# Output and down projections in five column pieces of 410 and 408 instead of four of 512

## The chip, the core and the metric

The kernel runs on one core of a Trainium2 chip. The metric is the device time of one execution in microseconds (us), as the median of several runs. Next to it stands one profiled execution, from which all the rows below come. The engines are called PE (TensorE, the matrix multiplier), ACT (ScalarE), DVE (VectorE), POOL (GpSimd) and SP (SyncE, which issues the transfers of the weights); PEld is the part of TensorE that loads the stationary operand.

## The reference

Two layers of an encoder work on x, 256 rows of 2048 columns in float32. Cut to what matters here, one layer is

```python
h = rms_norm(x, attn_norm[l])
proj = jnp.einsum('bsd,de->bse', h, w_in[l])        # 2048 -> 4672 columns
...                                                 # three mixers a, b, c of 4, 6 and 6 heads of 128
y = jnp.concatenate([rms_norm(ya, g_a), rms_norm(yb, g_b), rms_norm(yc, g_c)], axis=-1)
x = x + jnp.einsum('bse,ed->bsd', y, w_out[l])      # 2048 -> 2048
h = rms_norm(x, ffn_norm[l])
ff = jax.nn.silu(h @ w_gate[l]) * (h @ w_up[l])     # 2048 -> 5632, twice
x = x + ff @ w_down[l]                              # 5632 -> 2048
```

After the second layer a last rms_norm with the gain final_norm gives the output.

## The kernel before

**Units.** Every projection is cut into units (line 350). A unit is one weight matrix, a range of contraction tiles of 128 rows (`k0`, `nk`) and a range of output columns (`c0`, `n`, at most 512). `run_units` (line 353) works through all units of both layers in one list. It cuts a unit into granules of two contraction tiles, and a granule into twelve matmuls: each float32 weight is split into a high part `wh` and a low part `wl`, each activation likewise (`xh`, `xl` or `ah`, `al`), and of the four products three are kept, for two contraction tiles and two halves `t` of the 256 rows (lines 424 to 431). The stationary operand of a matmul is a 128x128 tile of activations, the moving operand a weight tile of `n` columns, and the result goes to `acc`, of which there are two sets. A new stationary tile is loaded for every matmul.

**Weights.** One load brings up to four contraction tiles of a unit (`load`, line 365) into one of three `raw` buffers, by SP's queue. `convert` (line 380) makes `wh` by a cast on ACT and `wl` by a subtraction on DVE, two granules ahead of the matmuls, into three buffers; the next load is issued when the last granule of a `raw` buffer is converted.

**Ends of units.** When a unit's last matmul has been issued, its evacuation waits for the next granule's conversion to be issued (`pend`, lines 411 to 413) and then runs: for the output projection (`ev_out`, line 878) and the down projection (`ev_down`, line 945) DVE adds `acc` to the columns of x, once for each `t`.

**The rest of the work** (attention, norms, transposes) is made of tasks. `pump` (line 215) puts them between the granules, by a planner's own costs and due times (`Pace`, line 37); what is ordered there at build time is the order on the engines. A norm of x is taken in four chunks of 512 columns (`norm_chunk`, line 328): each is transposed on PE, scaled and split on ACT and DVE, and squared on ACT. The norm before the gate and up projections starts from `ev_out` of mixer b (`m == 1`, the last of the three), the norm before the second layer from `ev_down` of the last group; the final norm instead takes each piece as it comes (`final_part`, line 332): squares on ACT, then a multiplication by the gain on DVE.

**Sizes of what the change touches.** The output projection has 4, 6 and 6 contraction tiles for the three mixers, in the order a, c, b (line 888), each with four column pieces. The down projection has 44 contraction tiles in six groups, five of 8 and one of 4, each with four column pieces. In the second layer the last group has five, since its last 512 columns are cut in two (lines 968 and 969).

Of the kernel before, what the change touches and what calls it, by code (L numbers as in the profile page):

```python
# [13 lines left out]
ALU = mybir.AluOpType  # L14
# [6 lines left out]
D = 2048  # L21
DEPTH = 2
# [8 lines left out]
MAX_HEADS = 5  # L31
PE_SLACK = -800
READY_AHEAD = 250
QUEUE_AHEAD = 3000


# [80 lines left out]
def hybrid_encoder(tc, pools, a, out):  # L117
    pace = Pace()
    nc = Core(tc.nc, pace)
# [5 lines left out]
    gf = [None, None]  # L125
# [6 lines left out]
    x = const.tile([P, T, D], F32, name="x")  # L132
# [23 lines left out]
    def drop(name, i):  # L156
        slots[name].append((pace.mark, i))
# [17 lines left out]
    def temp(name, shape, dtype=F32):  # L175
        i = yield from take(name)
        return i, sp.tile(shape, dtype, name=f"{name}{i}", tag=f"{name}{i}", bufs=1)
# [10 lines left out]
    def finish(key):  # L188
        done[key] = pace.mark + Pace.HOP
# [15 lines left out]
    def due(task):  # L205
        now = pace.at["pe"]
        if task.engine == "pe":
            return task.ready <= now + PE_SLACK
        return task.ready <= now + READY_AHEAD and pace.at.get(task.engine, 0.0) <= now + QUEUE_AHEAD

# [35 lines left out]
    def start(gen, engine="pe", ready=None):  # L246
        prep.append(Task(gen, engine, max(pace.at["act"], pace.at["dve"]) + Pace.HOP if ready is None else ready))
# [11 lines left out]
    def inv_rms(dst, ss, width, n):  # L259
        ms = tiny.tile([P, 16], F32, name="ms", tag="ms", bufs=2)  # L260
        nc.vector.tensor_scalar(ms[:, :n], ss, 1.0 / width, EPS, ALU.mult, ALU.add)
        nc.gpsimd.tensor_tensor(dst, ms[:, :n], half[:, :n], ALU.pow)

    def small(name, n, bufs=2):
        return tiny.tile([P, n], F32, name=name, tag=name, bufs=bufs)
# [15 lines left out]
    def new_norm(gbase, key):  # L281
        n = Norm()
        n.gbase, n.key = gbase, key
        n.hi = [None] * 8
        n.lo = [None] * 8
        n.ss = tiny.tile([P, 10 if key == "final" else 8], F32, name=f"ss_{key}")
        n.parts = 0
        n.r = tiny.tile([P, 2], F32, name=f"r_{key}")
        n.left = 8
        return n  # L290
# [6 lines left out]
    def norm_end(n):  # L297
        tot = small("tot", 2)
        nc.vector.tensor_reduce(tot, n.ss.rearrange("p (t c) -> p t c", t=T), AX.X, ALU.add)
        inv_rms(n.r, tot, D, 2)  # L300
        finish((n.key, "r"))

    def norm_pair(n, kp):
        n.hi[kp] = sp.tile([P, 2, S], F32R, name=f"xh{kp}", tag=f"xh{kp}", bufs=1)
        n.lo[kp] = sp.tile([P, 2, S], F32R, name=f"xl{kp}", tag=f"xl{kp}", bufs=1)
        bank = yield from grab()
        for j in range(2):
            kt = 2 * kp + j
            for t in range(T):
                o = j * S + t * P  # L310
                nc.tensor.transpose(bank[1][:, o : o + P], x[:, t, kt * P : (kt + 1) * P], ident)
        yield "act"
        g = gT[:, n.gbase + 2 * kp : n.gbase + 2 * kp + 2]
        split_scaled(
            [(n.hi[kp][:, j], n.lo[kp][:, j], bank[1][:, j * S : (j + 1) * S], g[:, j : j + 1]) for j in range(2)]
        )
        give(bank)
        finish((n.key, kp))
        cur[0].ready += 2000
        yield "act"  # L320
        i, junk = yield from temp("pr", [P, T, S])
        square(n, kp // 2, kp % 2, junk.rearrange("p t s -> p (t s)"))
        drop("pr", i)
        if n.left == 0:
            yield "dve"
            norm_end(n)

    def norm_chunk(n, c, ready=None):
        for b in range(2):
            start(norm_pair(n, 2 * c + b), "pe", ready)  # L330

    def final_part(n, c0, w):
        i, junk = yield from temp("pr", [P, T, S])
        for t in range(T):
            nc.scalar.activation(
                junk.rearrange("p t s -> p (t s)")[:, :w], x[:, t, c0 : c0 + w], AF.Square,
                accum_out=n.ss[:, 5 * t + n.parts : 5 * t + n.parts + 1],
            )
        drop("pr", i)
        n.parts += 1  # L340
        if n.parts == 5:
            norm_end(n)
        for t in range(T):
            xs = x[:, t, c0 : c0 + w]
            nc.vector.tensor_mul(xs, xs, gf[c0 // 1024][:, c0 % 1024 // 512, c0 % 512 : c0 % 512 + w])


    units = []
# [1 line left out]
    def unit(w, k0, nk, c0, n, act, evac, need=None, evac_need=()):  # L350
        units.append((w, k0, nk, c0, n, act, evac, need, evac_need))
# [120 lines left out]
    def layer(l, nrm, next_norm):  # L472
        L = Norm()
# [5 lines left out]
        nh = (A_H, B_H, C_H)  # L479
        y_base = (0, A_H, A_H + B_H)  # L480
# [7 lines left out]
        def y_tiles(kt):  # L488
            i = kt // 8
            if L.y[i] is None:  # L490
                L.y[i] = tuple(
                    sp.tile([P, 8, S], F32R, name=f"a{s}{i}", tag=f"a{s}{i}", bufs=1) for s in "hl"
                )
            return L.y[i][0][:, kt % 8], L.y[i][1][:, kt % 8]
# [380 lines left out]

        fn = new_norm(G_FFN + 16 * l, f"ffn{l}")

        def ev_out(m, c):
            def f(acc):
                for t in range(T):  # L880
                    xs = x[:, t, c * 512 : (c + 1) * 512]
                    nc.vector.scalar_tensor_tensor(xs, acc[t], L.rm[m][:, t : t + 1], xs, ALU.mult, ALU.add)
                if m == 1:
                    norm_chunk(fn, c)

            return f

        for m in (0, 2, 1):
            for c in range(4):
                unit(  # L890
                    a["w_out"][l], y_base[m], nh[m], c * 512, 512,
                    lambda k, b=y_base[m]: y_tiles(b + k), ev_out(m, c),
                    lambda k, b=y_base[m]: ("y", l, b + k), (("rm", l, m),),
                )

# [7 lines left out]
        groups = [(0, 1), (2, 3), (4, 5), (6, 7), (8, 9), (10,)]  # L903
        F = Norm()
# [37 lines left out]

            return f

        def ev_down(g, c, c0, n):
            def f(acc):
                for t in range(T):
                    xs = x[:, t, c0 : c0 + n]
                    nc.vector.tensor_add(xs, acc[t][:, :n], xs)
                if g == len(groups) - 1:  # L950
                    if l + 1 < DEPTH:
                        norm_chunk(next_norm, c)
                    else:
                        start(final_part(next_norm, c0, n), "act")
                elif l + 1 == DEPTH and g == 0 and c == 0:
                    final_gain()

            return f
# [5 lines left out]

        def down(g):
            k0 = 4 * groups[g][0]
            cuts = [0, 512, 1024, 1536, 2048]
            if l + 1 == DEPTH and g == len(groups) - 1:
                cuts.insert(4, 1792)
            for c0, c1 in zip(cuts, cuts[1:]):  # L970
                unit(
                    a["w_down"][l], k0, 4 * len(groups[g]), c0, c1 - c0,
                    lambda k: (F.t[g][0][:, k], F.t[g][1][:, k]), ev_down(g, c0 // 512, c0, c1 - c0),
                    lambda k: ("ff", l, groups[g][0] + k // 4),
                )

        gu(0)
        for g in range(1, len(groups)):
            gu(g)
            down(g - 1)  # L980
        down(len(groups) - 1)


    norms = [new_norm(G_ATTN + 16 * l, f"attn{l}") for l in range(DEPTH)] + [new_norm(0, "final")]
    for l in range(DEPTH):
        layer(l, norms[l], norms[l + 1])
# [17 lines left out]
    def final_gain():  # L1004
        gf[:] = [nat(tag, 512) for tag in ("n2", "n3")]
        for i, g in enumerate(gf):
            src = a["final_norm"].unsqueeze(0)[:, i * 1024 : (i + 1) * 1024].to_broadcast([P, 1024])
            nc.sync.dma_start(g, src.rearrange("p (t n) -> p t n", t=T))
# [16 lines left out]
    for c in range(4):  # L1025
        xs = x[:, :, c * 512 : (c + 1) * 512]
# [72 lines left out]
```

## Time and profile before

| | |
|---|---|
| median of 3 runs | 2220.07 us (2219.35 to 2221.93) |
| the profiled execution's own time | 2221.58 us |
| its span, first to last instruction | 2219.8 us |
| instructions | 26883 |
| PE, DVE, ACT, POOL busy | 99%, 56%, 47%, 9% of the span |
| weights and other data read from memory | 399.50 MB |

A busy share of PE says only that some matmul was in flight, since matmuls overlap: what a matmul costs is read from the distance between the starts of two that follow each other. In a line of the timeline the first column is the start of the first instruction of a run of equal ones, the second the time from there to the end of the last, and "x4" their count; what stands in brackets is how long the engine was idle before, and what ended that.

### The profile page before, as it was taken

What the parts mean: (1) busy time and instruction counts of PE and PEld (TensorE: products, weight loads), DVE (VectorE), ACT (ScalarE), POOL (GpSimd) and SP (SyncE); (2) the same over time, 40 slices, a digit from 0 to 9 for tenths busy, and PEclk for the clock granted to TensorE, in tenths of its full rate; (3) what the DMA queues carried; (4) which work ended last, traced back from release to release, by engine and by line L of the source; (5) the groups of instructions that cost most, each with busy time, mean ns of one, the idle gap of its engine ahead of it and who ended that gap; (6) DMA issues with size and microseconds to landing.
All of it is one profiled execution on the core that took longest, in us unless ns stands there. A gap on an engine that the chain in (4) does not pass through costs nothing.

```text
span 2219.8 us, 26883 instructions
## 1 busy us (share of the span) xinstructions
PE 2192.1 (99%) x10486; PEld 1842.1 (83%) x10486; DVE 1244.8 (56%) x1468; ACT 1045.0 (47%) x1473; POOL 210.3 (9%) x323
## 2 busy tenths in 40 slices
PE   8999999999999999999999999999999999999997
PEld 7887988888888888888888889888888888888886
DVE  5556676444545455455655567664455455554555
ACT  6556545444344443444455555454444434444444
POOL 0425400000000000000004453000000000000000
PEclk9999999999999999999999999999999999999999
DMA  7544466565655555555555535565656556555553
GB/s 263 169 125 146 128 198 194 186 193 189 191 190 189 190 190 190 190 190 190 190 191 166 158 100 166 171 193 191 190 192 208 191 190 190 190 190 190 190 190 133
DMA packets 213295, 403.34 MB, mean 182 GB/s; under 512 B 6848, under 2 KB 28848, under 8 KB 213168
## 3 DMA queue, kind: packets, MB, share of 16 engines
q1 hardware_dynamic: 210416, 399.55, 56.3%
q10 hardware_dynamic: 2752, 2.07, 0.3%
q8 instruction: 82, 1.34, 0.2%
q14 instruction: 45, 0.37, 0.0%
HBM read 399.50 MB, written 2.10 MB: 181 GB/s over the span
## 4 chain that ended last, share of the span: by engine, by line
PE 64%; issue 33%; POOL 1%; DVE 1%; DMA 0%; ACT 0%; ACTq 0%; POOLq 0%; SPq 0%; DVEq 0%
PE acc L95 59%; PE side L95 5%; POOL trig_c L95 0%; DMA gc<-in_c_q_norm_dram 0%; POOL tb L95 0%; POOL ta L95 0%; POOL n L95 0%; DMA gains<-in_attn_norm_dram 0%; DVE wl L95 0%; ACT wh L95 0%; ACT pr L95 0%; DVE pr L95 0%; DVE qkl L95 0%; DVE nm L95 0%; ACT x L95 0%
## 5 line engine op out<-in xcount | busy, mean ns | idle before, releaser
L95 DVE TENSOR_TENSOR wl<-raw,wh 128x1024 fp32r<-128x1024 f32 (+3 forms) x786 | 938.4, 1194 | 822.8 <-ACT wh L95 787.9
L95 ACT CAST wh<-raw 128x1024 fp32r<-128x1024 f32 (+3 forms) x786 | 800.1, 1018 | 957.0 <-PE acc L95 941.3
L95 PE MATMUL acc<-wh,xl 128*128 128x512 f32 (+2 forms) x2112 | 545.3, 380 | 0.0
L95 PE MATMUL acc<-wl,xh 128*128 128x512 f32 (+2 forms) x2112 | 544.7, 380 | 0.0
L95 PE MATMUL acc<-wh,xh 128*128 128x512 f32 (+2 forms) x2112 | 543.5, 379 | 1.1 <-ACT wh L95 1.1
L95 PEld LDWEIGHTS acc<-wh,xh 128*128 128x128 f32 x2112 | 384.4, 189 | 73.6 <-ACT wh L95 1.5
L95 PEld LDWEIGHTS acc<-wh,xl 128*128 128x128 f32 x2112 | 385.6, 189 | 72.1
L95 PEld LDWEIGHTS acc<-wl,xh 128*128 128x128 f32 x2112 | 382.9, 189 | 70.6
L95 PE MATMUL acc<-wl,ah 128*128 128x512 f32 (+2 forms) x1032 | 276.2, 389 | 0.0
L95 PE MATMUL acc<-wh,ah 128*128 128x512 f32 (+2 forms) x1032 | 273.3, 387 | 0.0
L95 PE MATMUL acc<-wh,al 128*128 128x512 f32 (+2 forms) x1032 | 272.8, 386 | 0.0
L95 PEld LDWEIGHTS acc<-wh,al 128*128 128x128 f32 x1032 | 192.6, 188 | 38.7
L95 PEld LDWEIGHTS acc<-wh,ah 128*128 128x128 f32 x1032 | 192.2, 188 | 38.5
L95 PEld LDWEIGHTS acc<-wl,ah 128*128 128x128 f32 x1032 | 189.8, 188 | 35.9
L95 POOL TENSOR_TENSOR r_attn<-ms,half 128x2 f32<-128x2 f32 x2 | 1.4, 700 | 763.2 <-DVE ms L95 763.2
L95 POOL TENSOR_TENSOR r_final<-ms,half 128x2 f32<-128x2 f32 x1 | 0.8, 802 | 720.2 <-DVE ms L95 720.2
L95 ACT CAST ah<-side 128x512 fp32r<-128x512 f32 x44 | 25.8, 587 | 83.1 <-PE side L95 83.1
L95 DVE TENSOR_TENSOR x<-acc,x 128x512 f32<-128x512 f32 (+1 forms) x98 | 61.8, 672 | 1.2 <-PE acc L95 1.2
L95 DVE TENSOR_TENSOR al<-side,ah 128x512 fp32r<-128x512 f32 x44 | 30.4, 692 | 55.0 <-ACT ah L95 55.0
L95 PE MATMUL side<-ident,n 128*128 128x128 f32 x336 | 50.4, 274 | 6.6 <-POOL n L95 6.3
L95 PEld LDWEIGHTS side<-ident,n 128*128 128x128 f32 x336 | 40.4, 139 | 16.1 <-POOL n L95 8.0
L95 POOL TENSOR_TENSOR n<-ta,tb 128x256 f32<-128x256 f32 (+1 forms) x48 | 39.4, 821 | 3.8
(112 smaller groups left out, 958.0 us busy)
## 6 DMA issues: line engine op xcount, KB each, us to landing
raw<-in_w_gate_dram SPq DMA_DIRECT2D x88, 1024.0 KB, 5.1
raw<-in_w_up_dram SPq DMA_DIRECT2D x88, 1024.0 KB, 5.1
raw<-in_w_down_dram SPq DMA_DIRECT2D x87, 1024.0 KB, 5.0
raw<-in_w_in_dram SPq DMA_DIRECT2D x55, 1024.0 KB, 5.0
raw<-in_w_out_dram SPq DMA_DIRECT2D x24, 1024.0 KB, 5.2
raw<-in_w_in_dram SPq DMA_DIRECT2D x26, 512.0 KB, 3.7
raw<-in_w_out_dram SPq DMA_DIRECT2D x16, 512.0 KB, 3.6
raw<-in_w_in_dram SPq DMA_DIRECT2D x8, 640.0 KB, 4.1
```

What stands on the lines that cost most here:

```text
L95: f(*args, **kw)
```

## The change

The output projection and the down projection take their 2048 columns in the pieces 0 to 410, 410 to 820, 820 to 1230, 1230 to 1640 and 1640 to 2048, in every group of both layers. Since the norms still go by chunks of 512 columns, a chunk is started by the piece that completes it (`whole`): the pieces 2, 3, 4 and 5 complete the chunks 1, 2, 3 and 4, and piece 1 completes none. In the final norm, the multiplication by the gain is cut where a piece crosses a multiple of 512.

```diff
+CUTS = (0, 410, 820, 1230, 1640, 2048)
...
+        edges = [c0] + [e for e in range(512, D, 512) if c0 < e < c0 + w] + [c0 + w]
         for t in range(T):
-            xs = x[:, t, c0 : c0 + w]
-            nc.vector.tensor_mul(xs, xs, gf[c0 // 1024][:, c0 % 1024 // 512, c0 % 512 : c0 % 512 + w])
+            for e0, e1 in zip(edges, edges[1:]):
+                xs = x[:, t, e0:e1]
+                nc.vector.tensor_mul(xs, xs, gf[e0 // 1024][:, e0 % 1024 // 512, e0 % 512 : e0 % 512 + e1 - e0])
...
+        def whole(c1, c0):
+            return [c for c in range(4) if c0 < (c + 1) * 512 <= c1]
+
-        def ev_out(m, c):
+        def ev_out(m, c0, n):
             def f(acc):
                 for t in range(T):
-                    xs = x[:, t, c * 512 : (c + 1) * 512]
-                    nc.vector.scalar_tensor_tensor(xs, acc[t], L.rm[m][:, t : t + 1], xs, ALU.mult, ALU.add)
+                    xs = x[:, t, c0 : c0 + n]
+                    nc.vector.scalar_tensor_tensor(xs, acc[t][:, :n], L.rm[m][:, t : t + 1], xs, ALU.mult, ALU.add)
                 if m == 1:
-                    norm_chunk(fn, c)
+                    for c in whole(c0 + n, c0):
+                        norm_chunk(fn, c)
...
         for m in (0, 2, 1):
-            for c in range(4):
+            for c0, c1 in zip(CUTS, CUTS[1:]):
                 unit(
-                    a["w_out"][l], y_base[m], nh[m], c * 512, 512,
-                    lambda k, b=y_base[m]: y_tiles(b + k), ev_out(m, c),
+                    a["w_out"][l], y_base[m], nh[m], c0, c1 - c0,
+                    lambda k, b=y_base[m]: y_tiles(b + k), ev_out(m, c0, c1 - c0),
...
-        def ev_down(g, c, c0, n):
+        def ev_down(g, c0, n):
...
-                        norm_chunk(next_norm, c)
+                        for c in whole(c0 + n, c0):
+                            norm_chunk(next_norm, c)
...
-                elif l + 1 == DEPTH and g == 0 and c == 0:
+                elif l + 1 == DEPTH and g == 0 and c0 == 0:
...
-            cuts = [0, 512, 1024, 1536, 2048]
-            if l + 1 == DEPTH and g == len(groups) - 1:
-                cuts.insert(4, 1792)
-            for c0, c1 in zip(cuts, cuts[1:]):
+            for c0, c1 in zip(CUTS, CUTS[1:]):
                 unit(
                     a["w_down"][l], k0, 4 * len(groups[g]), c0, c1 - c0,
-                    lambda k: (F.t[g][0][:, k], F.t[g][1][:, k]), ev_down(g, c0 // 512, c0, c1 - c0),
+                    lambda k: (F.t[g][0][:, k], F.t[g][1][:, k]), ev_down(g, c0, c1 - c0),
```

## Rows read from the trace of the kernel before

**Rows 1.** The timeline of PE inside a down projection of the first layer.

```profile
597.02 1.07 PE L95 MATMUL acc<-wh,al 128*128 128x512 f32 x4
...
600.64 1.07 PE L95 MATMUL acc<-wl,ah 128*128 128x512 f32 x4
```

**Rows 2.** The timeline of PE: 384-column, 320-column and 256-column pieces.

```profile
85.94 0.85 PE L95 MATMUL acc<-wh,al 128*128 128x384 f32 x4
...
88.71 0.85 PE L95 MATMUL acc<-wl,ah 128*128 128x384 f32 x4
...
251.20 0.75 PE L95 MATMUL acc<-wl,xh 128*128 128x320 f32 x4
251.79 0.75 PE L95 MATMUL acc<-wh,xh 128*128 128x320 f32 x4
...
2203.25 0.64 PE L95 MATMUL acc<-wh,al 128*128 128x256 f32 x4
...
2208.05 0.64 PE L95 MATMUL acc<-wl,ah 128*128 128x256 f32 x4
```

**Rows 3.** The page's costliest groups: matmuls of the projections after the first.

```profile
L95 PE MATMUL acc<-wh,ah 128*128 128x512 f32 (+2 forms) x1032 | 273.3, 387 | 0.0
```

**Rows 4.** Stretches: busy time (instructions) of PE, PEld, DVE, ACT, POOL; PEclk, DMA share, GB/s.

```profile
250.00:280.00 30.00, 30.00 (x247) 29.99 (x246) 23.99 (x48) 19.17 (x44) 17.05 (x23) 1.00 0.50 142
600.00:690.00 90.00, 90.00 (x402) 74.52 (x401) 43.62 (x40) 38.15 (x39) 0.00 (x0) 1.00 0.59 187
```

**Rows 5.** Groups by form: conversions and adds of different widths.

```profile
L95 DVE TENSOR_TENSOR wl<-raw,wh 128x1024 fp32r<-128x1024 f32 x710 | 874.8, 1232 | 776.5 <-ACT wh L95 770.6 <-PE acc L95 4.6
...
L95 ACT ACTIVATE pr<-x 128x512 f32<-128x512 f32 x38 | 24.0, 639 | 0.1
...
L95 DVE TENSOR_TENSOR wl<-raw,wh 128x768 fp32r<-128x768 f32 x8 | 7.7, 962 | 12.3 <-PE acc L95 9.8 <-ACT wh L95 2.5
...
L95 ACT CAST wh<-raw 128x768 fp32r<-128x768 f32 x8 | 6.7, 840 | 10.9 <-PE acc L95 10.8
...
L95 ACT ACTIVATE pr<-x 128x256 f32<-128x256 f32 x4 | 1.7, 418 | 2.1 <-DVE x L95 2.1
```

**Rows 6.** The timeline of ACT in the first layer's output projection (one of an even pattern).

```profile
321.34 1.06 ACT L95 CAST wh<-raw 128x1024 fp32r<-128x1024 f32 x1 [1.66 <-PE acc L95]
```

**Rows 7.** The timeline at the first layer's end, where the next norm's chunks come in.

```profile
1104.26 1.04 PE L95 MATMUL side<-ident,x 128*128 128x128 f32 x8
...
1104.89 1.57 ACT L95 ACTIVATE xh<-side,gT 128x256 fp32r<-128x256 f32 x4 [0.30 <-PE side L95]
...
1105.77 1.28 DVE L95 TENSOR_TENSOR x<-acc,x 128x512 f32<-128x512 f32 x2
...
1106.97 1.65 DVE L95 SCALAR_TENSOR_TENSOR xl<-side,gT,xh 128x256 fp32r<-128x256 f32 x4
```

**Rows 8.** The DMA issues, with KB of one and the median us to landing.

```profile
raw<-in_w_down_dram SPq DMA_DIRECT2D x87, 1024.0 KB, 5.0
...
raw<-in_a_w_uq_dram SPq DMA_DIRECT2D x4, 768.0 KB, 4.4
```

**Rows 9.** The timeline of the end, all engines.

```profile
2208.61 0.76 DVE L95 TENSOR_TENSOR x<-acc,x 128x256 f32<-128x256 f32 x2 [1.21 <-PE acc L95]
2209.07 0.42 ACT L95 ACTIVATE pr<-x 128x256 f32<-128x256 f32 x1 [0.92 <-DVE x L95]
2209.28 0.75 DVE L95 TENSOR_TENSOR x<-x,n 128x256 f32<-128x256 f32 x2
...
2210.15 0.16 DVE L95 TENSOR_REDUCE tot<-ss_final 128x2 f32<-128x10 f32 x1
...
2210.42 0.76 DVE L95 TENSOR_TENSOR x<-x,n 128x256 f32<-128x256 f32 x2
2210.59 0.80 POOL L95 TENSOR_TENSOR r_final<-ms,half 128x2 f32<-128x2 f32 x1 [720.24 <-DVE ms L95]
```

**Rows 10.** A stretch of the second layer's attention, columns as in the stretches above.

```profile
1255.00:1300.00 45.00, 39.70 (x239) 34.95 (x237) 25.61 (x48) 26.65 (x74) 26.92 (x48) 0.92 0.51 167
```

## The prediction, made before the changed kernel ran

> **What bounds the kernel now.** I began with the busy shares of the page: PE is busy nearly all of the span, every other engine about half of it or less. That alone proves little, since overlapping matmuls keep PE "busy" even where it starts them late. So the second view is the timeline of PE, and in it the distance between starts. In a down projection with pieces of 512 columns, 16 matmuls lie between the two starts shown: 3.62 us, 226 ns each to the rounding of the rows [rows 1]. The other widths in this kernel give 2.77 us for 16 at 384 columns (173 ns), 0.59 us for 4 at 320 (147 to 148 ns) and 4.80 us for 40 at 256 (120.0 ns) [rows 2]. These four lie on one line: from 256 to 512 columns the step grows by 106.7 ns, which is 0.4167 ns a column, one column per cycle at 2.4 GHz; what is left at zero columns is 120.0 - 106.7 = 13.3 ns. The line gives 226.7, 173.3, 146.7 and 120.0. So **each matmul costs its columns and 13.3 ns more, whatever its width**. In the 90 us window the granted clock is 1.00 and PE is busy all through [rows 4]; ACT's conversions of weights stand idle before each start until a matmul frees their buffer, 1.66 us out of each 2.72 us [rows 6]. The supply waits for PE, not PE for the supply. In the stretches that the change touches, time is therefore the number of matmuls times their step.
>
> **The matmuls, removed and added.** One form of the three products counts 1032 matmuls outside the w_in, gate and up projections [rows 3]. By the code that is 2 layers x 2 halves x (16 tiles x 4 pieces of w_out + 44 x 4 of w_down + 16 of the low-rank projections) = 1024, and 8 more because the last group of the second layer already has five pieces. Taking off the low-rank 64 leaves 968, for three products 2904 matmuls. Of these 48 have 256 columns (4 tiles x 2 halves x 3 products x 2 pieces) and 2856 have 512: 2856 x 226.67 + 48 x 120.0 = 653.1 us. After the change there are 60 tiles x 2 halves x 3 products x 2 layers = 720 for each piece: 2880 of 410 columns and 720 of 408. By the line a step is (410 + 32) / 2.4 = 184.2 ns, or 183.3 ns at 408: 530.4 + 132.0 = 662.4 us. **The difference is 9.3 us**, which is just 696 more matmuls at 13.3 ns, since the columns are the same. No row has a width that isn't a multiple of 64, so the step at 410 is not seen. The rows on either side are 384 (173.3 ns) and 512 (226.7 ns), and one column per cycle at all four widths leaves no room for less than the line; above it, if PE took columns in sixteens, 410 would cost what 416 does, 186.7 ns. I take the line and keep the other as the upper bound, +9.6 us (2880 x 2.5 ns + 720 x 3.3 ns). The loads of the stationary operand, one a matmul, fit into the 120 ns step, so they don't bind at 184.
>
> The Trainium skill bears on this. Its page "TensorE: Matmul & The Clock Gate", section "Back-to-back issue gap", puts the isolated warm step at columns / 2.4 plus 2.5 ns. By that 512 columns would take 215.8 ns and the 696 matmuls would cost 1.7 us. The trace has 226.7 ns at 512 and 120.0 ns against the rule's 109.2 at 256, so here the row decides.
>
> **Conversions.** A granule's two tiles become 820 elements a partition instead of 1024. From 768 to 1024 DVE's subtraction goes from 962 to 1232 ns [rows 5], so 820 take about 1.02 us; ACT's cast takes 840 ns at 768 and 1.06 us at 1024 [rows 5, 6], so about 0.88. A granule of twelve matmuls lasts 2.21 us instead of 2.72. There are more granules, but both engines keep half of each free, and the cast still starts 4.4 us before its granule (two granules ahead) and ends with 3.5 us in hand. I cost this at nothing; PE's two granules in stock hide it.
>
> **Evacuations and norm chunks.** There are 17 more units: 3 in each layer's output projection and 6 in its down projection, less 1. The adds go on DVE while PE fills the other set of `acc`. The tightest place is the last group of the first layer with its 24 matmuls a piece, where the norm's chunks come in: per chunk 8 transposes on PE, 1.57 us of scaling on ACT, 1.65 us on DVE, and 1.28 us of adds a piece [rows 7], besides two squares of 0.64 us [rows 5] and their read-outs. On ACT I get 2 x 0.88 + 1.57 + 2 x 0.64 = 4.6 us a piece and the read-outs on top, on DVE 2 x 1.02 + 1.1 + 1.65 = 4.8, against 4.4 us of matmuls and 0.8 of transposes [rows 7] on PE. So ACT is level with PE for three pieces, no more than that; what it loses, a few tenths of a us, comes out of the 3.5 us in hand. Chunk 4 is still started by the last piece, and its columns are wanted only at the seventh granule of the next unit, over 16 us later, so the wait for it stays hidden. I cost this at nothing too; without that stock it would be up to 1 us in each layer.
>
> **Loads.** A load becomes 820 KB in rows of 1640 bytes. At 1024 KB it lands in 5.0 us, at 768 KB in 4.4 [rows 8]; I expect about 4.5. It is issued when a buffer is free and wanted two loads later: 8.8 us instead of 10.9. SP issues 31 loads more in all (5 a layer for w_out, 11 and 10 for w_down), and its queue holds nothing that is wanted sooner: nothing for that. Narrower rows use the DMA engines somewhat more: 0.50 for 142 GB/s where pieces are narrow, 0.59 for 187 where they are wide [rows 4], 11% more a byte, and half of that is not enough to matter. Rows that start at multiples of 1640 bytes are in no row of this trace.
>
> **The end.** PE's last piece is in the sum above; what follows it has 408 columns instead of 256. After the last matmul come DVE's adds, ACT's two squares, the reduction 1.54 us after the adds began, POOL's power and the scaling [rows 9]. The square goes from 418 to 639 ns between 256 and 512 columns [rows 5], so +0.13 us each, and the first add +0.16 us: +0.42 by ACT. On DVE the two adds take +0.32 us, and the multiplications of the piece before go between them and the reduction; they had just room (2209.28 to 2210.03 against 2210.15) and become four on 820 columns instead of two on 512, about +0.35 us. So the reduction comes 0.4 to 0.7 us later: **I take 0.6**. The last multiplications grow from 0.76 to 1.08 us, beside POOL's 0.80 us [rows 9], hidden to within 0.1 us.
>
> **The sum** is 9.3 + 0.6 = 9.9 us. On the profiled execution, 2221.6 us of its own time, that is 2231.5. That execution was 1.5 us above the median of the runs, so I predict 2220.1 + 9.9 = **2230.0 us**. A measurement of this kernel tells about 0.2% from no change, 4.4 us; the sum is twice that.
>
> **The rivals.** *Wide columns in PE*: it takes 410 as 416, so +9.6 on top, 2239.6 us. Nothing speaks for it but the lack of a row; chance 0.06. Its mark would be a step of 186.7 ns. *Transfers*: if rows off a round start took 1.7 times the engine time (0.59 x 1.7 = 1.0), the loads would become the bound; at twice, 18% of 662 us, some 2350 us. Against it stands that the load only shifts its start; 0.03. *The fixed part is smaller than it seems*: most of the 13.3 ns belongs to something that isn't paid per matmul, so 1.7 us and the end's 0.6, 2222.4 us, no change. Four widths on a line speak against it; 0.05. *Not slower, by the attention of the second layer*: there PE idles 5.3 of 45 us and its clock is granted at 0.92 on average [rows 10], so 8% of 45 us is another 3.6 us lost. The planner orders that work by its own clock, which the 410-column pieces of the first layer shift; if that removed both losses, 8.9 us, the result would be 2221.1, and with luck elsewhere in that layer less than before. It decides only if nearly the whole loss goes. The work of that stretch and the units around it are not touched, and the planner's clock moves for all engines together; 0.06, with 0.02 of it below no change by over 0.2%. That leaves **0.80 for the forecast**, whose own range is 2227 to 2233: the 0.4 to 0.7 us at the end, and the 2.6 us by which runs of one kernel differ.
>
> **The range** is 2226 to 2240: it takes in the forecast and the first rival, the upper bound of the unknown step, and leaves out 0.14 of the other three and the tails. Slower by over 0.2% (above 2224.5) is the forecast and the first two rivals: 0.89. Within 0.2% is the third rival and most of the fourth, 0.09; faster the rest, 0.02.
>
> **What would show it.** In the profile of the changed kernel the matmuls outside w_in, gate and up should count 1264 a product, and 16 starts in a down projection 2.95 us apart: 184 ns each. ACT should still wait for matmuls before its conversions, about 1.2 us of each 2.21. Loads of 820 KB should land in about 4.5 us. The last start of a matmul should come about 9.3 us later than before (2208.05 is the start of its last four), and from the adds to the reduction it should take 2.1 us instead of 1.54. The prediction is wrong if the step at 410 is off the line, if ACT's conversions wait for a DMA, if PE starts wait for `wh` in the 410 pieces, or if the time before the first 410 piece differs between the two kernels.

## The result and the profile after

The changed kernel takes 2236.36 us in the median (2235.75 to 2237.92) against 2219.78 us (2219.35 to 2221.93): **16.6 us more, ratio 1.0074 with a 95% interval of 1.0056 to 1.0091**. The prediction was 2230.0 us, 9.9 more, with a range of 2226 to 2240. The direction and the range held, but the forecast's own range, 2227 to 2233, was missed: 6.7 us of the size were not in it.

The first place to look is the groups of matmuls on the page of the changed kernel, which answer to [rows 3].

```profile
PE 2206.2 (99%) x11182; PEld 1969.3 (88%) x11182; DVE 1256.4 (56%) x1566; ACT 1054.7 (47%) x1531; POOL 209.2 (9%) x323
...
L96 PE MATMUL acc<-wh,ah 128*128 128x410 f32 (+3 forms) x1264 | 288.8, 350 | 0.0
...
L96 PEld LDWEIGHTS acc<-wh,ah 128*128 128x128 f32 x1264 | 235.0, 190 | 2.1
```

The count is the predicted 1264 a product, and 11182 matmuls in all are 696 more than the 10486 before. So the term to doubt is the price of one, the step from one start to the next. The timeline of PE in the first down projection has it: 16 matmuls of 410 columns between the first two rows, 16 of 408 between the others.

```profile
577.17 0.91 PE L96 MATMUL acc<-wh,ah 128*128 128x410 f32 x4
...
580.16 0.91 PE L96 MATMUL acc<-wh,al 128*128 128x410 f32 x4
...
597.31 0.90 PE L96 MATMUL acc<-wh,ah 128*128 128x408 f32 x4
...
600.27 0.90 PE L96 MATMUL acc<-wh,al 128*128 128x408 f32 x4
```

2.99 us for 16 are 186.9 ns to the rounding of the rows; over all matmuls of 410 that have only their like around them it is 186.7. At 408 it is 2.96 / 16 = 185.0 ns. The line had promised 184.2 and 183.3. With 2880 and 720 matmuls that is 537.6 + 133.2 = 670.8 us instead of 662.4. One might take that step for the time of the loads of the stationary operand, whose mean of 190 ns is near that step. But they take 187 to 192 ns in the projections at every width, and the starts still lie 180.0 ns apart at 400 columns and 120.0 at 256 and 264.

Does that come out in the stretches? From the first matmul of a projection to the first of the next, an output projection took 97.12 us after and 95.05 before (2.07 more, twice), a down projection of eight tiles 45.58 and 44.49 (1.09 more, eight times), the last two groups of the first layer with the w_in unit behind them 138.68 and 137.10 (1.58), those of the second layer to the last matmul's start 67.75 and 66.44 (1.31). Together 15.8 us; the steps alone say 17.7. Other matmuls share these stretches; where the 1.9 us between lie is not shown.

The gate and up projections stand still (88.01 us a pair before, 88.05 after). The supply is what the prediction said. These are ACT's timeline in the first down projection, two DMA issues, and two stretches with the columns of [rows 4], the first inside a down projection and the second in the gate and up projections.

```profile
572.15 0.88 ACT L96 CAST wh<-raw 128x820 fp32r<-128x820 f32 x1 [1.36 <-PE acc L96]
574.39 0.88 ACT L96 CAST wh<-raw 128x820 fp32r<-128x820 f32 x1 [1.36 <-PE acc L96]
```

```profile
raw<-in_w_down_dram SPq DMA_DIRECT2D x88, 820.0 KB, 4.6
...
raw<-in_w_down_dram SPq DMA_DIRECT2D x22, 816.0 KB, 4.6
```

```profile
559.00:603.00 44.00, 44.00 (x241) 43.91 (x240) 26.37 (x32) 18.10 (x21) 0.00 (x0) 1.00 0.62 202
604.00:690.00 86.00, 86.00 (x385) 71.17 (x384) 41.89 (x38) 36.12 (x38) 0.00 (x0) 1.00 0.60 188
```

The casts take 0.88 us and still wait for a matmul 1.36 us out of each 2.24; the loads land in 4.6 us, and the clock stays granted at 1.00. In the list of waits no conversion waits for a load of w_out or w_down. Rows that start at odd multiples of 1640 bytes cost nothing that the time shows: 0.62 of the DMA engines for 202 GB/s is no more a byte than 0.60 for 188.

The end, as the timeline has it, answers to [rows 9].

```profile
2222.37 1.07 DVE L96 TENSOR_TENSOR x<-acc,x 128x408 f32<-128x408 f32 x2 [1.67 <-PE acc L96]
2222.99 0.54 ACT L96 ACTIVATE pr<-x 128x408 f32<-128x408 f32 x1 [2.97 <-DVE x L96]
...
2224.32 0.16 DVE L96 TENSOR_REDUCE tot<-ss_final 128x2 f32<-128x10 f32 x1 [0.88 <-ACT pr L96]
```

From the first add to the reduction it is 1.95 us against 1.54, 0.41 more; POOL's power took 0.16 us more besides, and from the last matmul's start to the end of the span it is 12.0 us against 11.4. 15.8 + 0.6 = 16.4 us, and 16.6 were measured.

The two profiled executions differ by less, 14.4 us. What is missing lies in code that the change leaves alone: the w_in units of the first layer took 183.1 us before and 182.1 after, those of the second 183.7 and 182.0. In the second layer, the stretch that answers to [rows 10] is this one.

```profile
1262.00:1307.00 45.00, 39.99 (x251) 35.31 (x250) 26.61 (x51) 27.81 (x77) 27.48 (x49) 0.96 0.52 171
```

PE's idle time is what it was (5.0 us against 5.3), but the clock was granted at 0.96 instead of 0.92, that is 3.4 us at the lower level of 1.2 GHz instead of 6.8, which is worth 1.7 us. The first layer shows the like before anything of the change has run, 3.4 us instead of 6.8. In the ten traces of this case its w_in units, whose code all the kernels share, took 182.0 to 183.6 us, so that much is the luck of one execution; those of the second layer took 181.1 to 183.7, to either side of the two above.

### The profile page after: what moved, and what is told of

The parts are those of the page before. It is cut to its first block, busy times and chain, and to the rows that moved or that the text cites. A ratio compares the mean times of both kernels' runs of the same rounds, so it can differ in the third digit from the quotient of the medians.

```text
span 2234.2 us, 28627 instructions
## 1 busy us (share of the span) xinstructions
PE 2206.2 (99%) x11182; PEld 1969.3 (88%) x11182; DVE 1256.4 (56%) x1566; ACT 1054.7 (47%) x1531; POOL 209.2 (9%) x323
## 3 DMA queue, kind: packets, MB, share of 16 engines
q10 hardware_dynamic: 2752, 2.07, 0.3%
## 4 chain that ended last, share of the span: by engine, by line
PE 64%; issue 33%; POOL 1%; ACT 1%; DVE 0%; DMA 0%; POOLq 0%; ACTq 0%; SPq 0%
PE acc L96 59%; PE side L96 5%; DMA gc<-in_c_q_norm_dram 0%; POOL trig_c L96 0%; POOL tb L96 0%; POOL ta L96 0%; POOL n L96 0%; ACT wh L96 0%; DMA gains<-in_attn_norm_dram 0%; DVE wl L96 0%; ACT pr L96 0%; DVE pr L96 0%; DVE qkl L96 0%; ACT xh L96 0%; ACT x L96 0%
## 5 line engine op out<-in xcount | busy, mean ns | idle before, releaser
L96 DVE TENSOR_TENSOR wl<-raw,wh 128x1024 fp32r<-128x1024 f32 (+4 forms) x844 | 947.7, 1123 | 838.3 <-ACT wh L96 801.1
L96 ACT CAST wh<-raw 128x1024 fp32r<-128x1024 f32 (+4 forms) x844 | 809.2, 959 | 982.4 <-PE acc L96 970.2
L96 PE MATMUL acc<-wl,ah 128*128 128x410 f32 (+3 forms) x1264 | 289.1, 350 | 0.0
L96 PE MATMUL acc<-wh,ah 128*128 128x410 f32 (+3 forms) x1264 | 288.8, 350 | 0.0
L96 PE MATMUL acc<-wh,al 128*128 128x410 f32 (+3 forms) x1264 | 288.0, 349 | 0.0
L96 PEld LDWEIGHTS acc<-wh,al 128*128 128x128 f32 x1264 | 236.0, 190 | 1.3
L96 PEld LDWEIGHTS acc<-wh,ah 128*128 128x128 f32 x1264 | 235.0, 190 | 2.1
L96 PEld LDWEIGHTS acc<-wl,ah 128*128 128x128 f32 x1264 | 234.6, 190 | 1.1
L96 DVE TENSOR_TENSOR x<-acc,x 128x410 f32<-128x410 f32 (+1 forms) x120 | 64.1, 576 | 1.7 <-PE acc L96 1.7
```

What stands on the lines that cost most here:

```text
L96: f(*args, **kw)
```

## The experiments

All times over before are against runs of the kernel before on the same chip.

### The parts alone

The output projection alone has the old pieces in `down`, the down projection alone the old ones for w_out:

```diff
         def down(g):
...
-            for c0, c1 in zip(CUTS, CUTS[1:]):
+            cuts = [0, 512, 1024, 1536, 2048]
+            if l + 1 == DEPTH and g == len(groups) - 1:
+                cuts.insert(4, 1792)
+            for c0, c1 in zip(cuts, cuts[1:]):
```

```diff
-        for m in (0, 2, 1):
-            for c0, c1 in zip(CUTS, CUTS[1:]):
+            for c0, c1 in ((0, 512), (512, 1024), (1024, 1536), (1536, 2048)):
```

> Only the output projection in pieces of 410 and 408, the down projection as before. By the stretches of the changed kernel's trace the two output projections grew by 2.07 us each: 4.1 us over before, ratio 1.0019, if nothing of the change acts across stretches. If the planner's order in the second layer's attention moves with the pieces of the first, the stretch of w_in units in the second layer would differ by more than that from the first layer's, and the time would be off 4.1 us by some us either way.

> Only the down projection in pieces of 410 and 408, the output projection as before. By the stretches of the changed kernel's trace: 8 x 1.09 + 1.61 + 1.31 for the groups and 0.64 for what follows the last matmul, 12.3 us over before, ratio 1.0055; with the output projection alone it should add up to the whole change, 16.4 us. If the parts don't add up, something acts across them.

The output projection alone took 2224.75 us against 2220.31, 4.4 more, ratio 1.0019 (1.0010 to 1.0028); the down projection alone 2232.25, 11.9 more, ratio 1.0053 (1.0040 to 1.0065). They add up to 16.4, against 16.6 for both. So nothing acts across stretches that these runs, each good to 2 or 3 us, can show, and the planner's order in the second layer, my fourth rival, plays no part that they show.

### Is it the width? A multiple of 16

```diff
-CUTS = (0, 410, 820, 1230, 1640, 2048)
+CUTS = (0, 416, 832, 1248, 1664, 2048)
```

> Theory S: the moving columns of a matmul are taken in sixteens, so 410 costs what 416 does, (416 + 32) / 2.4 = 186.7 ns. Four pieces of 416 and one of 384 then cost 2880 x 186.67 + 720 x 173.33 = 662.4 us against 653.1 before: +9.3 us, and +0.5 at the end for a last piece of 384 instead of 256, so 9.8 us over before, ratio 1.0044, some 6.5 us under the pieces of 410; the starts in a 384 piece lie 173.3 ns apart and in a 416 piece 186.7. Rival F: what the pieces of 410 cost beyond the line of the four widths comes from having five units instead of four (their ends, loads and conversions); then this kernel stands as high as the one with 410, 16.6 us over before, ratio 1.0075. Rival R: it comes from rows that start off a multiple of 64 bytes; then the time is that of the line, and a step in a 416 piece is 186.7 ns as well, so the two pieces of the next run's groups that lie on and off such a start tell S and R apart.

2232.12 us against 2220.31: 11.8 more, ratio 1.0056 (1.0042 to 1.0070). That is below the change, so rival F is out in its plain form. It is 2 us above theory S, whose 1.0044 the interval still holds, so the step has to decide. The timeline of PE in a piece of 416, 64 matmuls apart:

```profile
575.43 0.92 PE L96 MATMUL acc<-wh,al 128*128 128x416 f32 x4
...
587.48 0.92 PE L96 MATMUL acc<-wl,ah 128*128 128x416 f32 x4
```

12.05 / 64 = 188.3 ns. The piece that S names as the round size costs *more* than the 410 that it was to explain, and 1.6 ns more than the line. S falls.

### A map of widths

Each group of the down projection gets pieces of its own:

```diff
+WIDTHS = {
+    (0, 0): (416, 416, 416, 416, 384),
+    (0, 1): (400, 402, 404, 406, 436),
+    (0, 2): (408, 412, 414, 418, 396),
+    (0, 3): (448, 480, 432, 424, 264),
+    (0, 4): (498, 504, 508, 294, 244),
+    (1, 0): (420, 422, 426, 428, 352),
+    (1, 1): (386, 388, 390, 392, 492),
+    (1, 2): (408, 410, 410, 410, 410),
+    (1, 3): (320, 328, 336, 344, 352, 368),
+    (1, 4): (440, 444, 456, 464, 244),
+}
...
-            for c0, c1 in zip(CUTS, CUTS[1:]):
+            cuts = [0]
+            for n in WIDTHS.get((l, g), [q - p for p, q in zip(CUTS, CUTS[1:])]):
+                cuts.append(cuts[-1] + n)
+            for c0, c1 in zip(cuts, cuts[1:]):
```

> One look at the step of a matmul at many widths: ten groups of the down projection each take other pieces, from 244 to 508 columns; the rest stays as with 410. Theory S: a staircase, (width rounded up to 16, plus 32) / 2.4: 386, 388, 390, 392 and 396 columns would all take 180.0 ns (as 400), 402 to 414 all 186.7, 418 to 432 193.3, and only 320, 336, 352, 368, 384, 400, 416, 432, 448, 464, 480 lie on the line of the trace before. Line: 386 takes 174.2, 402 takes 180.8, 414 takes 185.8, 418 takes 187.5 ns. Rival R (row starts): 416 from column 832 and 410 from column 408 differ by where they start, and the step follows the start rather than the width: the groups with the pieces in the order 408, 410, 410, 410, 410 have other starts and would show other steps.

In the timeline of PE of this kernel the first rows of two pieces that follow each other lie 48 matmuls apart, so a step is their difference divided by 48 (between pieces 2 and 5 nothing else is mixed in). The line is the prediction's, (columns + 32) / 2.4.

```profile
702.78 0.90 PE L108 MATMUL acc<-wh,ah 128*128 128x402 f32 x4
...
711.60 0.90 PE L108 MATMUL acc<-wh,ah 128*128 128x404 f32 x4
...
720.36 0.91 PE L108 MATMUL acc<-wh,ah 128*128 128x406 f32 x4
...
863.21 0.88 PE L108 MATMUL acc<-wh,ah 128*128 128x396 f32 x4
...
871.85 1.09 PE L108 MATMUL acc<-wh,xh 128*128 128x512 f32 x4
...
970.55 1.04 PE L108 MATMUL acc<-wh,ah 128*128 128x480 f32 x4
...
980.96 0.93 PE L108 MATMUL acc<-wh,ah 128*128 128x432 f32 x4
...
990.36 0.92 PE L108 MATMUL acc<-wh,ah 128*128 128x424 f32 x4
...
999.48 0.65 PE L108 MATMUL acc<-wh,ah 128*128 128x264 f32 x4
...
1005.24 1.09 PE L108 MATMUL acc<-wh,xh 128*128 128x512 f32 x4
...
1060.56 1.07 PE L108 MATMUL acc<-wh,ah 128*128 128x504 f32 x4
...
1071.44 1.06 PE L108 MATMUL acc<-wh,ah 128*128 128x508 f32 x4
```

| columns | step, ns | line | off the line |
|---|---|---|---|
| 264 | 120.0 | 123.3 | -3.3 |
| 396 | 180.0 | 178.3 | +1.7 |
| 402 | 183.8 | 180.8 | +2.9 |
| 404 | 182.5 | 181.7 | +0.8 |
| 424 | 190.0 | 190.0 | 0.0 |
| 432 | 195.8 | 193.3 | +2.5 |
| 480 | 216.9 | 213.3 | +3.5 |
| 504 | 226.7 | 223.3 | +3.3 |

It is no staircase: 404 is cheaper than 402, 504 costs what 512 does, and 432 and 480, multiples of 16, stand above the line. It is the line with a misfit of -3.3 to +3.5 ns in these rows (+5.0 at the worst of the other widths, 456 at 208.3 ns), that goes up and down with the width. The four widths of the kernel before, 256, 320, 384 and 512, lie on the line, and so do 336, 368 and 400 of this map; that is why the line had looked exact. Rival R falls too: the pieces of 410 that follow a 408 start at other places of the rows than those of the change and have the same 186.7 ns.

### Where the columns start

The pieces of 416 and 384 again, and in each group another shift of the weights' columns in their buffers or of the sums in the accumulators:

```diff
+SHIFT = {
+    (0, 0): (0, 0), (0, 1): (2, 0), (0, 2): (4, 0), (0, 3): (8, 0), (0, 4): (16, 0),
+    (1, 0): (0, 0), (1, 1): (0, 2), (1, 2): (0, 8), (1, 3): (0, 16), (1, 4): (8, 8),
+}
...
-            split(hi[:, :, :n], lo[:, :, :n], raws[ld][:, 2 * h : 2 * h + 2, :n])
+            split(hi[:, :, o : o + n], lo[:, :, o : o + n], raws[ld][:, 2 * h : 2 * h + 2, :n])
...
-                            acc[t][:, :n], ops[j][lw][:, t * P : (t + 1) * P], rw[:, j, :n], start=first, stop=last
+                            acc[t][:, po : po + n], ops[j][lw][:, t * P : (t + 1) * P], rw[:, j, o : o + n], start=first,
+                            stop=last,
```

> The width map put 400 columns at 180.0 ns, on the line, 410 at 186.7 and 416 at 188.2, both above it, and no smooth staircase. This look takes the pieces 416 and 384 and shifts, group by group of the down projection, where the weights' columns start in their buffers (by 2, 4, 8 or 16 columns) and where the sums start in the accumulators (by 2, 8 or 16), with the first group of each layer unshifted. Theory W: what a matmul costs above the line goes by its width alone: all groups show 188.2 and 173.3 to 173.7 ns. Rival A: it goes by the places that the moving columns fill, in blocks of 8 or 16 columns from the start of the buffer: a shift by 2, 4 or 8 adds up to a block, up to 6.7 ns, to both widths, a shift by 16 nothing. Rival P: it goes by the accumulators' places: the groups shifted there differ, and those with shifted weights don't.

In the timeline of PE, pairs of rows 64 matmuls apart: unshifted, weights by 2, weights by 4, sums by 2.

```profile
572.90 0.92 PE L101 MATMUL acc<-wh,ah 128*128 128x416 f32 x4
...
584.95 0.92 PE L101 MATMUL acc<-wh,al 128*128 128x416 f32 x4
...
705.82 0.93 PE L101 MATMUL acc<-wl,ah 128*128 128x416 f32 x4
...
718.11 0.93 PE L101 MATMUL acc<-wh,ah 128*128 128x416 f32 x4
...
838.83 0.91 PE L101 MATMUL acc<-wh,al 128*128 128x416 f32 x4
...
850.78 0.91 PE L101 MATMUL acc<-wl,ah 128*128 128x416 f32 x4
...
1811.06 0.92 PE L101 MATMUL acc<-wh,al 128*128 128x416 f32 x4
...
1823.11 0.92 PE L101 MATMUL acc<-wl,ah 128*128 128x416 f32 x4
```

They give 188.3, 192.0, 186.7 and 188.3 ns. The shift of the sums does nothing, by 8 and 16 neither (188.3); the shift of the weights does, and by 16 it is gone again (188.3 over that group and the unshifted one behind it). At 384 a shift by 4 takes the step from 173.3 to 175.5. So W and P fall, and A holds in so far as the place of the moving columns matters; but not its count of blocks, by which every shift of 2, 4 or 8 had to make 416 dearer: 4 made it cheaper, and so did 8 (186.7 ns in both groups that have it).

Place and width do not settle it either. These rows lie further ahead in the unshifted group, before the first transposes that come in between its matmuls, 12 matmuls apart:

```profile
559.24 0.91 PE L101 MATMUL acc<-wh,al 128*128 128x416 f32 x4
...
561.48 0.91 PE L101 MATMUL acc<-wh,al 128*128 128x416 f32 x4
```

That is 186.7 ns, and behind the transposes 188.3, in every unshifted group of eight tiles, here and in the kernel with pieces of 416 above; with the shift by 8 it is 193.3 and then 186.7. So a step also depends on what ran before, and the figures for 416 columns, shifted and not, are those behind the transposes. Whether the transposes themselves change it is not shown. In the change the 410 have 186.7 ns on both sides.

The same edit with `CUTS` as in the change, and other shifts:

```diff
+SHIFT = {
+    (0, 0): (0, 0), (0, 1): (2, 0), (0, 2): (4, 0), (0, 3): (6, 0), (0, 4): (16, 0),
+    (1, 0): (8, 0), (1, 1): (10, 0), (1, 2): (12, 0), (1, 3): (14, 0), (1, 4): (0, 0),
+}
...
```

> The pieces of the change, 410 and 408, with the weights' columns in their buffers shifted, group by group of the down projection, by 0, 2, 4, 6, 16 (first layer) and 8, 10, 12, 14, 0 (second layer) columns. With 416 columns the step went with such a shift (188.2 ns unshifted, 192.0 by 2, 186.7 by 4, 187.1 by 8, 188.3 by 16) and not with a shift of the sums. Theory A, the misfit goes by where the moving columns start, modulo 16: at 410 and 408 the step differs from 186.7 and 185.0 ns in some of the groups shifted by 2 to 14 by one to several ns, and comes back to those values by 16. Rival W, at 410 it goes by the width alone: 186.7 in every group. If a shift brings 410 down to the line, 184.2 ns, the misfit of the change could have been removed without other widths.

At 410 columns the step was 186.7 ns unshifted and by 2, 8, 10, 14 and 16, 185.4 by 4, 185.3 by 6 and 185.8 by 12. At 408 a shift by 2 made 190.0 of 185.0: its 48 matmuls are the ones between these rows.

```profile
729.94 0.92 PE L101 MATMUL acc<-wh,ah 128*128 128x408 f32 x4
...
739.06 1.08 PE L101 MATMUL acc<-wh,xh 128*128 128x512 f32 x4
```

A holds again, weakly, and no shift brings 410 down to the line. By what rule width, place and what ran before make the misfit stays open.

### The count alone, on the line

With widths that fit, the price of a matmul more can be had by itself. Five pieces as in the change, and six (five in the last group of the second layer):

```diff
-CUTS = (0, 410, 820, 1230, 1640, 2048)
+CUTS = (0, 512, 912, 1312, 1712, 2048)
```

```diff
-CUTS = (0, 410, 820, 1230, 1640, 2048)
+CUTS = (0, 368, 704, 1040, 1376, 1712, 2048)
+LAST = (0, 512, 912, 1312, 1712, 2048)
...
-            for c0, c1 in zip(CUTS, CUTS[1:]):
+            cuts = LAST if l + 1 == DEPTH and g == len(groups) - 1 else CUTS
+            for c0, c1 in zip(cuts, cuts[1:]):
```

> Five pieces as in the change, but of 512, 400, 400, 400 and 336 columns, widths that lay on the line in the width map. Theory L: the same 696 matmuls more as in the change, at 13.3 ns each, 9.3 us, and 0.3 at the end: 9.6 us over before, ratio 1.0043, 7 us under the pieces of 410; what the change cost beyond that is the misfit of its widths, 2.5 ns at 410 and 1.7 at 408. Rival U: five units instead of four cost 16.6 us whatever their widths; then this kernel stands with the change, ratio 1.0075.

> Six pieces of 368 and 336 columns, widths that lay on the line in the width map (five of 512, 400 and 336 in the last group of the second layer): 4296 matmuls instead of 2904 in the two projections. Theory L (13.3 ns for each matmul more, at widths on the line): 1392 x 13.33 = 18.6 us, and 0.3 at the end for a last piece of 336 instead of 256: 18.9 over before, ratio 1.0085. Rival U, units cost something beside their matmuls (loads, conversions, evacuations, order): the more units, the more over 18.9; at twice the 17 units of the change, by what the five pieces on the line show above 9.6 us, doubled.

Five pieces took 2229.23 us against 2221.84: 7.4 more, ratio 1.0037 (1.0024 to 1.0049). The interval holds theory L's 1.0043 and leaves out rival U's 1.0075. The timeline of PE: three pieces of 400, 144 matmuls, lie between these rows, 25.92 us or 180.0 ns each.

```profile
569.35 0.89 PE L96 MATMUL acc<-wh,ah 128*128 128x400 f32 x4
...
595.27 0.77 PE L96 MATMUL acc<-wh,ah 128*128 128x336 f32 x4
```

Six pieces took 2238.13: 16.3 more, ratio 1.0076 (1.0062 to 1.0090), with L's 1.0085 inside. By the stretches of the two traces, taken as above, the projections grew by 9.1 and 17.2 us, where L says 9.3 and 18.6. Twice the added matmuls cost nearly twice the time, and in the traces nothing is left over for the units.

## Why the prediction was right, and where it was too small

**What bounds the kernel** was read rightly: PE's starts set the time in all that the change touches, and ACT, DVE and the loads had room at 820 elements, with the casts' 0.88 us, the loads' 4.6 us and the waits forecast to within 0.2 us.

**The matmuls.** Their number was exact, and the price of one more holds where the width fits: 9.1 us in the trace of the kernel with 512, 400 and 336, against 9.3. The rival by which most of the 13.3 ns isn't paid per matmul (no change, 0.05) fell with it. The Trainium skill's page "TensorE: Matmul & The Clock Gate", section "Back-to-back issue gap", has 2.5 ns beside the columns for an isolated matmul at the full clock; the 1.7 us that the prediction worked out from it are an estimate, and these runs show 13.3 ns and 9.1 us. **The step that failed is the step time at 410 columns**, taken from the line as 184.2 ns. It is 186.7, and 185.0 instead of 183.3 at 408: 8.4 us more over 3600 matmuls, of which 6.5 show in the stretches. By the prediction's own signs that makes it wrong at this point, as it had named a step off the line as one. Another of its signs came up by luck: the first piece of 410 began 0.8 us sooner than the same place before, by the clock of the first layer. The bound "no less than the line" was no law either: 264 columns came out under it.

**The first rival** (410 as 416, chance 0.06) had named the very step, 186.7 ns, and with it the upper bound of the range; the forecast's own ended at 2233, below the 2236 measured. Its mechanism is not the cause: 416 itself mostly takes 188.3, and 408, which it put at 186.7, takes 185.0. So the range held by luck: the bound was right by its size, not by its reason. Four widths that are all multiples of 64 could not tell a line from a line with a misfit in between, and 0.06 was too little for that.

**Conversions, evacuations, loads** were costed at nothing, and the kernel with five pieces on the line leaves nothing for them. Where ACT was to be level with PE, in the first layer's last groups, the stretch grew by 1.58 us and the steps alone say 1.80, so nothing was lost there either. **Transfers** as the bound (0.03) fell: the rows' odd starts don't show. **The attention of the second layer** (0.06) did differ by 1.7 us between the two profiles, with 3.4 us less at the lower clock, but the first layer's differed too, by 1.0, and the parts alone add up to the whole.

**The end** was put at 0.6 us, and is 0.6: 0.4 by ACT's squares, as worked out. DVE's multiplications of the piece before, which I expected to push the reduction further, had run earlier and were not in the way; the rest of it is POOL's power, 0.96 us instead of 0.80.

## What to carry to other kernels

Where PE is the bound and every matmul has a stationary operand of its own, count matmuls before columns: each cost 13.3 ns beside its columns at every width that fits, so four pieces of 512 were cheaper than every division into five or six that was run, by 7 us at the least. If a width must be smaller, take one whose step has been seen in a trace (here 256, 320, 336, 368, 384, 400) rather than an even division of the total: 410 and 416 cost 2.5 and 1.6 ns a matmul beyond that. In the change this came to two thirds as much again as the added matmuls. A line through the widths that a trace happens to hold is no measurement of the ones between.

## What the runs showed that was not expected

The distance between matmuls is not a smooth function of the number of columns: 264 take 120.0 ns, the same as 256; 504 take 226.7, the same as 512; 402 take longer than 404. It moves by up to 5 ns with the place of the moving columns in their buffer (408 columns: 185.0 ns at the start, 190.0 two columns further on) and not with the place of the sums. With width and place the same it can still change within a piece (416 columns: 186.7 ns before the first transposes, 188.3 behind). In a piece of 408 it repeats in fours, 187, 184, 182 and 187 ns, one for each of two contraction tiles and two halves of the rows.
